# Twelve rotary units that scale at the end on ScalarE, and one operand's splits fenced later, in a two-layer encoder

## The chip, the cores and the metric

The program runs on one core of one Trainium2 chip. The metric is the device time of one execution in microseconds. One execution of the kernel before was also profiled; its lines are what the prediction reads. Engines are named as in the profile: PE (matrix products), PEld (its weight loads), DVE (vector), ACT (scalar, activations), POOL (GpSimd), SP (which issues most of the DMAs).

## The reference, cut to what matters

Two layers over 1024 tokens of 1024 features, in float32. Each layer: RMS norm, one input projection, several attention groups (and a cross-attention to 256 memory tokens), a SiLU gate, an output projection, a residual. The first hunk concerns group A of layer 0, whose queries and keys are normalised for each head and then rotated; the second the output projection of layer 1.

```python
qa = rope_2d(rmsnorm(qa.reshape(B, S, A_HEADS, HEAD_DIM), q_norm_a[e]), grid_row, grid_col)
ka = rope_2d(rmsnorm(ka.reshape(B, S, A_KV, HEAD_DIM), k_norm_a[e]), grid_row, grid_col)
...
def rmsnorm(x, g):
    xf = x.astype(jnp.float32)
    y = xf * lax.rsqrt(jnp.mean(xf * xf, axis=-1, keepdims=True) + EPS)
    return (y * g.astype(jnp.float32)).astype(x.dtype)
...
def _rotate_axis(xa, ang):
    x1, x2 = jnp.split(xa, 2, axis=-1)
    return jnp.concatenate([x1 * c - x2 * s, x1 * s + x2 * c], axis=-1)
...
x = x + y @ w_out_odd[o]
```

The inverse root is one number for each token and head, and the rotation is linear, so the root may be multiplied in before or after it.

## The kernel before, in words

Every matrix product is made of three: an operand is split into a high part (rounded to the product's format, a copy on ACT) and a low part (the operand minus the high part, on DVE or POOL), and high x high, high x low and low x high are added up in a PSUM bank. So each weight tile and each moving operand passes ACT and then DVE or POOL before PE can use it. In the profile `wraw` is a loaded weight, `wh` and `wl` its parts.

The phases follow each other: the preparation (0 to about 145 us: group A's projections, the memory's keys and values, roots), layer 0's attention and output projection, the front of layer 1, layer 1's attention, and layer 1's output projection (from about 1340 us to the end). The instructions are written in program order, but a planner orders them for each engine when the program is built: it simulates the engines, takes ready instructions by priority, which is the program's order changed by the offsets in `AHEAD`, and respects fences, `issue_after(x)`, which keep an instruction behind `x` on that engine's queue. The order is then fixed for each engine, and waits on semaphores do the rest.

The preparation projects group A in units of 256 tokens: four units (k0 to k3) of keys, two heads by two blocks of 128 tokens, that is 4 roots and 256 columns, and eight units of queries (q0 to q7), four heads by two blocks, 8 roots and 512 columns. `a_unit` makes a projection in a bank of PSUM tag `pj` (five banks; the keys' are copied to SBUF tiles `x` first). `rope` then squares it on ACT (`rt1`, two buffers), sums each head on DVE, takes the root (`inv_sqrt`: ACT's Sqrt, then a reciprocal and a step of refinement, four small DVE instructions), multiplies the projection by the root (L890, tile `rqn`), multiplies that by the cosine table (L893) and, half by half, the sine table (L895, tile `rt2`, one buffer), and adds the two on POOL (L898, tile `rp`, two buffers). The sum is kept as `self.rotated`, behind which POOL's first weight splits of layer 0 are fenced. One unit later PE transposes `rp` (`back`) and the result is split. The memory values of layer 1 (L597) run between, on two more `pj` banks.

The output projection multiplies in blocks with seven products of sums, Strassen's way, which take in turn the operands `y11`, `t1`, `t2`, `t3`, `y22`, `y21` and `t4`. `y_parts` loads an operand's six tiles (`SP`) and splits them, each ACT copy and DVE difference behind the fence `after`, a pair (`self.high`, the last weight's high copy, and `self.added`, the last addition of a product to the residual). For layer 1 (`last`) the third operand `t3` lies in tiles H, the fourth `y22` in tiles with the tags P, P, q, q, v, of which P is an alias of k. At `t3` the fence for `y22` is taken right after t3's own splits are written, before t3's weights:

```python
        y = self.y_parts(yd, tags["y"][3], "t3", after, self.fetched if last else None)
        after = self.high, self.added
```

In the loop that follows, each of four products (18 matrix products of 512 columns each) reads two weight tiles of 384 columns, made by `weights` through `w_parts`, whose low parts alternate between DVE and POOL; `closed(i)` loads a residual and adds a bank of the first product to it. The printed functions carry the line numbers of the profile.

Of the kernel before, what the change touches and what calls it, by code (L numbers as in the profile page):

```python
# [13 lines left out]
OP = mybir.AluOpType  # L14
# [50 lines left out]
class Trunk:  # L65
# [802 lines left out]
    def rope(self, src, heads, tables, q):  # L868


        nc = self.nc
        n = 2 * heads
        w = n * 64
        bs = slice(2 * q, 2 * q + 2)
        cg, sg = tables
        s4 = src.rearrange("p b (h d) -> p b h d", d=64)
        t1 = self.st("rt1", [128, 512])[:, :w]
        t4 = t1.rearrange("p (b h d) -> p b h d", b=2, d=64)
        nc.scalar.activation(t4, s4, AF.Square)
        ss = self.st("rss", [128, 8])[:, :n]  # L880
        sv = ss.rearrange("p (b h) -> p b h", b=2)
        nc.vector.tensor_reduce(ss, t1.rearrange("p (a d) -> p a d", d=64), axis=AX.X, op=OP.add)
        big = int(heads == 4)
        nc.vector.scalar_tensor_tensor(sv, sv, 1.0 if big else 1.0 / 64, self.e2[:, big, bs][:, :, None].to_broadcast([128, 2, heads]),
                                       op0=OP.mult, op1=OP.add)
        y = self.inv_sqrt(ss, n)
        yv = y.rearrange("p (b h) -> p b h", b=2)
        qn = self.st("rqn", [128, 512])[:, :w]
        q4 = qn.rearrange("p (b h d) -> p b h d", b=2, d=64)
        nc.vector.tensor_tensor(q4, s4, yv[:, :, :, None].to_broadcast([128, 2, heads, 64]), op=OP.mult)  # L890
        u = self.st("rt2", [128, 512])[:, :w]
        u4 = u.rearrange("p (b h d) -> p b h d", b=2, d=64)
        nc.vector.tensor_tensor(t4, q4, cg[:, bs, None, :].to_broadcast([128, 2, heads, 64]), op=OP.mult)  # L893
        for o, i in ((0, 32), (32, 0)):
            nc.vector.tensor_tensor(u4[:, :, :, o:o + 32], q4[:, :, :, i:i + 32],  # L895
                                    sg[:, bs, None, o:o + 32].to_broadcast([128, 2, heads, 32]), op=OP.mult)
        rp = self.st("rp", [128, 512])[:, :w]
        self.rotated = nc.gpsimd.tensor_tensor(rp, t1, u, op=OP.add)  # L898
        return rp.rearrange("p (b g n) -> p b g n", b=2, n=128)

    def back(self, rp, h, l):
# [424 lines left out]
    def out_project(self, w, sd, yd, res, done, tags, banks, first, begun, last=False):  # L1326
# [4 lines left out]
        nc = self.nc  # L1331
# [3 lines left out]
        def weights(i, kind, us=(0, 1)):  # L1335

            src = sd[i][:, "3124".index(kind[1]), :] if kind[0] == "s" else w[i if kind[1] == "1" else 4 + i][:, 768 * (kind[2] == "2"):]
            for c in (cut[u] for u in us):
                with self.ahead("w"):
                    raw = self.st("wraw", [128, UNIT * 128], pool=self.base, bufs=4)[:, :384]  # L1340
                    self.fetched = nc.sync.dma_start(raw, src[:, c])
                    yield self.w_parts(raw, self.either())

        def product(y, bank, ws, start, cols=slice(0, 512), ks=range(6)):
            for u, (h, l) in enumerate(ws):
                for k in (k for k in range(3) if 3 * u + k in ks):
                    for e, (s, m) in enumerate(((h, 0), (h, 1), (l, 0))):
                        last = nc.tensor.matmul(bank, s[:, k, :], y[3 * u + k][m][:, cols],  # L1348
                                                start=start and u + k + e == 0, stop=u == 1 and k + e == 4,
                                                skip_group_check=True)  # L1350
            return last
# [19 lines left out]
        def residual(x, nt, half):  # L1371
            with self.tc.issue_after(self.fetched.ins) if last else nullcontext():
                nc.sync.dma_start(x, res[nt][:, 512 * (2 - half):512 * (3 - half)])

        def plus(x, p, op=OP.add):
            self.added = nc.vector.tensor_tensor(x, x, p, op=op)

        def square(x, k):

            sq = self.st(self.square_tag if k else "vt", [128, 512])  # L1380
            nc.scalar.activation(sq, x, AF.Square)
            if 0 < k < apart:
                nc.gpsimd.tensor_tensor(sums[0], sums[0], sq, op=OP.add)
            else:
                sums.append(sq)
# [11 lines left out]
        def closed(i):  # L1397
            residual(at(c22, i), 4 + i, 2)
            with self.ahead("sink"):
                plus(at(c22, i), yb[i])  # L1400
# [10 lines left out]
        y = self.y_parts(yd, tags["y"][1], "t1")  # L1411
        for i in products(y, yb, "s1", True, ready, *([opened] if last else [])):
            if not last:
                closed(i)
            if i == 1:
                after = self.high, self.added

        y = self.y_parts(yd, tags["y"][2], "t2", turn)
# [6 lines left out]
        y = self.y_parts(yd, tags["y"][3], "t3", after, self.fetched if last else None)  # L1425
        after = self.high, self.added
        for i in range(4):
            ws = list(weights(i, "s3")) if last else weights(i, "s3")
            if last:
                closed(i)  # L1430
            product(y, xb[i], ws, False)
            residual(at(c21, i), 4 + i, 1)
            with self.ahead("sink"):
                plus(at(c22, i), xb[i])
                plus(at(c21, i), xb[i])
                square(at(c22, i), i)

        y = self.y_parts(yd, tags["y"][4], "y22", after)
        after = self.high, self.added
# [9 lines left out]
        y = self.y_parts(yd, tags["y"][5], "y21", after)  # L1449
        after = self.high, self.added  # L1450
# [15 lines left out]
        y = self.y_parts(yd, tags["y"][6], "t4", after)  # L1466
# [799 lines left out]
```

## Time and profile before

| | |
|---|---|
| median of 3 runs | 1481.07 us |
| lowest, highest | 1480.27, 1485.23 us |
| the profiled execution | 1483.22 us |
| its span, first to last instruction | 1481.4 us |
| PE busy | 1462.3 us, 99% |
| DVE, ACT, POOL busy | 70%, 57%, 44% |
| granted clock of PE, mean | 0.995 |

In the views below, a row of the waits reads: who waited, for whom, microseconds in total, number of times, longest. A row of a timeline or of the chain reads: start, length, engine, line, instruction, tiles out<-in, count; in square brackets the idle time before it and what ended it. A row of busy time by stage reads: length, busy time (and instructions) of PE, PEld, DVE, ACT and POOL, granted clock, share of the DMA engines, GB/s. A row of one line's instructions reads: count, shortest/median/longest duration in ns, first and last start, shapes. A DMA row ends with the median time from issue to landing. Products in PE overlap, so the starts of two neighbours show their true distance, not their durations.

### The profile page before, as it was taken

The numbers are of one execution on the slowest core, as the hardware profiler recorded it, in microseconds if no ns is written. First come the engines' busy times: TensorE is split into PE (matmuls) and PEld (weight loads), VectorE is DVE, ScalarE is ACT, GpSimd is POOL, SyncE is SP. The second block draws the span as 40 slices with busy tenths as digits, with TensorE's granted clock in tenths as the row PEclk, the third lists the DMA queues.
The fourth block names the chain that finished last, engine by engine and source line by source line (L and its number), as shares of the span: only waits on it lengthen the run. The fifth ranks groups of instructions, "written<-read, shape, count | busy, mean of one in ns | idle before, by whom it ended". The sixth has DMA issues, their size and how long they took to land.

```text
span 1481.4 us, 24750 instructions
## 1 busy us (share of the span) xinstructions
PE 1462.3 (99%) x8049; PEld 1257.4 (85%) x8049; DVE 1035.0 (70%) x2125; ACT 838.4 (57%) x1877; POOL 645.1 (44%) x766
## 2 busy tenths in 40 slices
PE   9999999999999999999999999999999999999997
PEld 8998888988888888888888877888888888888786
DVE  6787777777766678776687866654457777787674
ACT  7733665556655356654544444444456777776453
POOL 1223668566765646553450000002325556764354
PEclk9999999999999999999999999999999999999999
DMA  8966335334342524388553434567575567789844
GB/s 279 324 153 181 118 114 169 121 121 138 116 139 83 195 78 142 104 270 308 188 179 127 145 133 143 154 166 276 201 268 172 187 206 255 249 249 325 284 141 141
DMA packets 171809, 271.87 MB, mean 184 GB/s; under 512 B 15648, under 2 KB 92704, under 8 KB 170656
## 3 DMA queue, kind: packets, MB, share of 16 engines
q1 hardware_dynamic: 171248, 270.20, 56.6%
q8 instruction: 64, 1.05, 0.3%
q14 instruction: 65, 0.53, 0.1%
q10 hardware_dynamic: 432, 0.09, 0.0%
HBM read 174.28 MB, written 83.89 MB: 174 GB/s over the span
## 4 chain that ended last, share of the span: by engine, by line
PE 88%; DVE 4%; DMA 3%; ACT 2%; issue 1%; SPq 1%; POOL 1%; POOLq 0%; DVEq 0%; ACTq 0%
PE pj L242 16%; PE pj L62 12%; PE x L1648 7%; PE tr L133 6%; PE pv L1080 4%; PE y L1648 4%; PE pv L62 3%; PE s L62 3%; PE pj L1348 3%; PE tr L62 3%; PE sa L1348 3%; PE pv L1648 2%; PE tr L1348 2%; PE sa L1046 2%; PE sa L1047 2%; PE s L1348 2%
## 5 line engine op out<-in xcount | busy, mean ns | idle before, releaser
L549 DVE TENSOR_TENSOR pl<-tr,ph 128x512 fp32r<-128x512 f32 (+2 forms) x352 | 204.4, 594 | 45.5 <-ACT ph L125 43.5
L242 PE MATMUL pj<-H,wh 128*128 128x512 f32 x704 | 233.5, 412 | 0.5 <-DVE vt L313 0.2
L125 ACT ACTIVATE ph<-tr 128x512 fp32r<-128x512 f32 (+2 forms) x352 | 176.6, 522 | 99.9 <-PE tr L133 78.0
L158 POOL TENSOR_SCALAR wh<-wraw 128x512 fp32r<-128x512 f32 x48 | 30.2, 631 | 270.0 <-PE x L1648 232.9
L125 ACT ACTIVATE wh<-wraw 128x384 fp32r<-128x384 f32 (+1 forms) x163 | 88.8, 553 | 103.3 <-PE pj L1348 17.6
L242 PE MATMUL pj<-H,wl 128*128 128x512 f32 x352 | 139.0, 395 | 0.0
L242 PEld LDWEIGHTS pj<-H,wh 128*128 128x128 f32 x704 | 120.2, 189 | 18.3 <-issue 0.6
L62 PE MATMUL pj<-H,wh 128*128 128x512 f32 x384 | 121.0, 396 | 0.0
L133 PE MATMUL tr<-ident,P 128*128 128x128 f32 x752 | 115.5, 273 | 0.7 <-DVE pl L549 0.3
L1133 POOL TENSOR_SCALAR pn<-pn,st 128x384 f32<-128x384 f32 (+1 forms) x128 | 72.7, 570 | 97.6 <-DVE st L1132 56.5
L1295 POOL TENSOR_TENSOR wl<-wraw,wh 128x384 fp32r<-128x384 f32 x56 | 63.2, 1131 | 98.7 <-ACT wh L125 88.5
L1131 ACT ACTIVATE pn<-pn,st 128x384 f32<-128x384 f32 (+1 forms) x128 | 75.1, 587 | 39.4 <-DVE st L1128 37.8
L133 PEld LDWEIGHTS tr<-ident,P 128*128 128x128 f32 x752 | 88.9, 140 | 9.3 <-POOL P L732 1.6
L1052 ACT ACTIVATE P<-sa,st 128x1024 f32<-128x1024 f32 x64 | 71.5, 1117 | 34.3 <-PE tr L133 19.6
L1054 POOL TENSOR_SCALAR P<-P,st 128x1024 f32<-128x1024 f32 x64 | 74.5, 1166 | 31.3 <-DVE st L1053 31.3
L1051 DVE TENSOR_REDUCE st<-sa 128x1 f32<-128x1024 f32 x64 | 77.6, 1219 | 7.8 <-PE sa L1047 6.8
L62 PE MATMUL s<-k,q 128*128 128x384 f32 (+1 forms) x352 | 81.2, 327 | 0.0
L242 PEld LDWEIGHTS pj<-H,wl 128*128 128x128 f32 x352 | 66.2, 188 | 15.1
L62 PE MATMUL pj<-H,wl 128*128 128x512 f32 x192 | 75.6, 394 | 0.0
L160 POOL TENSOR_TENSOR wl<-wraw,wh 128x512 fp32r<-128x512 f32 x52 | 70.5, 1358 | 9.2 <-ACT wh L125 6.5
L62 PEld LDWEIGHTS pj<-H,wh 128*128 128x128 f32 x384 | 66.6, 188 | 5.4
L864 PE MATMUL pj<-ah,H 128*128 128x256 f32 x384 | 70.5, 282 | 0.0
(574 smaller groups left out, 4171.8 us busy)
## 6 DMA issues: line engine op xcount, KB each, us to landing
y<-yb SPq DMA_DIRECT2D x24, 512.0 KB, 4.1
wraw<-s SPq DMA_DIRECT2D x64, 192.0 KB, 4.3
wraw<-w_e SPq DMA_DIRECT2D x44, 256.0 KB, 3.4
k<-k SPq DMA_DIRECT2D x42, 256.0 KB, 5.8
s<-bias SPq DMA_DIRECT2D x56, 192.0 KB, 2.0
wq<-w_o SPq DMA_DIRECT2D x40, 256.0 KB, 3.4
y<-sg SPq DMA_DIRECT2D x18, 512.0 KB, 3.3
wraw<-w_o SPq DMA_DIRECT2D x36, 256.0 KB, 4.4
```

The lines of the kernel that those rows point to most:

```text
L62: return lambda *a, **k: self.tc.keep_in_program_order(getattr(self.engine, name)(*a, **k))
L125: return self.nc.scalar.activation(out, in_, AF.Copy, scale=scale)
L133: self.turned = self.fence = self.pe.transpose(o, i, self.ident)
L242: self.pe.matmul(a[:, :n], s[:, kt % UNIT, :], m, start=(kt == 0 and i == 0), stop=(kt == KT - 1 and i == 2))
L549: self.low = nc.vector.tensor_tensor(pl[:, :n], tr[:, :n], ph[:, :n], op=OP.subtract)
L1051: nc.vector.tensor_reduce(st[:, 0:1], s, axis=AX.X, op=OP.max, negate=True)
L1052: nc.scalar.activation(pt, s, AF.Exp, bias=st[:, 0:1], accum_out=st[:, 1:2])
L1054: self.normal = nc.gpsimd.tensor_scalar(pt, pt, st[:, 2:3], 0.5, op0=OP.mult, op1=OP.mult)
L1131: nc.scalar.activation(o, o, AF.Exp, bias=st[:, 0:1], scale=-1.0, accum_out=st[:, 2:3])
L1133: self.normal = normal = nc.gpsimd.tensor_scalar(o, o, st[:, 3:4], 0.5, op0=OP.mult, op1=OP.mult)
L1348: last = nc.tensor.matmul(bank, s[:, k, :], y[3 * u + k][m][:, cols], start=start and u + k + e == 0, stop=u == 1 and k + e == 4, skip_gro ...
L1648: self.last = nc.tensor.matmul(bank, ws[s][:, k, :], b[k][m], start=start and k + i == 0, stop=k == UNIT - 1 and i == 2, skip_group_check= ...
```

## The change

In `rope`, the tables multiply the raw projection `s4`; the multiplication by the root and the tile `rqn` for it go. The root is taken after the POOL sum in program order, and ACT multiplies each head and block of the sum (128 x 64) in place by its root: eight copies with a scale for a unit of queries, four for one of keys. `self.rotated` stays the POOL sum. The pool of `rqn` stays, since `rope_tables` uses it. In `out_project` the fence for `y22` is, for layer 1, taken again in the first turn of t3's loop, when the two weight tiles of that turn have been made.

```diff
         big = int(heads == 4)
         nc.vector.scalar_tensor_tensor(sv, sv, 1.0 if big else 1.0 / 64, self.e2[:, big, bs][:, :, None].to_broadcast([128, 2, heads]),
                                        op0=OP.mult, op1=OP.add)
-        y = self.inv_sqrt(ss, n)
-        yv = y.rearrange("p (b h) -> p b h", b=2)
-        qn = self.st("rqn", [128, 512])[:, :w]
-        q4 = qn.rearrange("p (b h d) -> p b h d", b=2, d=64)
-        nc.vector.tensor_tensor(q4, s4, yv[:, :, :, None].to_broadcast([128, 2, heads, 64]), op=OP.mult)
         u = self.st("rt2", [128, 512])[:, :w]
         u4 = u.rearrange("p (b h d) -> p b h d", b=2, d=64)
-        nc.vector.tensor_tensor(t4, q4, cg[:, bs, None, :].to_broadcast([128, 2, heads, 64]), op=OP.mult)
+        nc.vector.tensor_tensor(t4, s4, cg[:, bs, None, :].to_broadcast([128, 2, heads, 64]), op=OP.mult)
         for o, i in ((0, 32), (32, 0)):
-            nc.vector.tensor_tensor(u4[:, :, :, o:o + 32], q4[:, :, :, i:i + 32],
+            nc.vector.tensor_tensor(u4[:, :, :, o:o + 32], s4[:, :, :, i:i + 32],
                                     sg[:, bs, None, o:o + 32].to_broadcast([128, 2, heads, 32]), op=OP.mult)
         rp = self.st("rp", [128, 512])[:, :w]
         self.rotated = nc.gpsimd.tensor_tensor(rp, t1, u, op=OP.add)
+        y = self.inv_sqrt(ss, n)
+        for i in range(n):
+            self.copy(rp[:, i * 64:i * 64 + 64], rp[:, i * 64:i * 64 + 64], y[:, i:i + 1])
         return rp.rearrange("p (b g n) -> p b g n", b=2, n=128)
...
         for i in range(4):
             ws = list(weights(i, "s3")) if last else weights(i, "s3")
             if last:
+                if i == 0:
+                    after = self.high, self.added
                 closed(i)
             product(y, xb[i], ws, False)
```

## The prediction

> **What bounds the kernel now.** I read the page's busy times first, then the waits of PE, then busy time by stage, and last the chain of waits and the timelines of the two places that the diff touches.
>
> ```profile
> span 1481.4 us, 24750 instructions
> PE 1462.3 (99%) x8049; PEld 1257.4 (85%) x8049; DVE 1035.0 (70%) x2125; ACT 838.4 (57%) x1877; POOL 645.1 (44%) x766
> ```
>
> PE is idle for 1481.4 - 1462.3 = 19.1 us in all, so an edit that leaves PE's work as it is can win only from this and from stretches where PE ran slowly. The waits of PE say where:
>
> ```profile
> PE pj L1348 <- ACT wh L125: 2.0, 1, 2.0
> ...
> PE pj L597 <- DVE wl L160: 1.3, 3, 0.8
> ...
> PE pj L597 <- DVE rqn L890: 0.8, 1, 0.8
> ...
> PE tr L133 <- POOL rp L898: 0.4, 1, 0.4
> ```
>
> The first is the longest wait of PE, and it lies in the output projection that the second hunk edits. The other three (1.3 + 0.8 + 0.4 = 2.5 us) lie in the preparation, where the rotary units run. By stage:
>
> ```profile
> 74.00:111.00 37.00, 36.25 (x285) 34.43 (x284) 31.80 (x86) 14.44 (x33) 9.73 (x8) 1.00 0.63 154
> 111.00:148.00 37.00, 35.66 (x209) 30.54 (x209) 26.69 (x57) 13.02 (x25) 12.80 (x13) 1.00 0.65 181
> 1370.00:1407.00 37.00, 34.78 (x141) 27.25 (x140) 22.17 (x31) 16.14 (x32) 14.13 (x11) 0.95 0.85 284
> ```
>
> Columns: length, then PE, PEld, DVE, ACT, POOL busy, granted clock, DMA share. In the preparation DVE is busy for 31.8 of 37 us and ACT for 14.4: DVE is what PE waits for, and ACT has room. In the third row PE also lost clock (0.95).
>
> **Second hunk: the fourth operand's splits.** The chain of waits runs through ACT here:
>
> ```profile
> 1392.62 0.51 ACT wh L125
> 1393.13 1.04 ACT k L125 x2
> 1394.17 0.39 ACT q L125
> ...
> 1395.12 1.14 ACT v L125 x2
> 1396.26 0.58 ACT H L125 x2
> ...
> 1397.72 1.35 ACT wh L125 x3
> ...
> 1399.11 9.75 PE pj L1348 x34
> 1408.86 8.40 PE s L1348 x36
> ```
>
> k, q and v are the buffers of the fourth operand (y22); H is the third (t3), which the next product needs. The six copies of y22 fill ACT from 1393.13 to 1396.26, ahead of three copies of t3 and of the first weights of that product. Their fence is the weight copy of 1392.62, the last of the stage before; the edit makes it the second of the 1397.72 group, so the six go behind t3's copies and the weights that PE waits for. What PE lost, and how slowly it ran after:
>
> ```profile
> 1395.87 0.39 PE L1361 MATMUL s<-H,wl 128*128 128x512 f32 x1
> 1398.28 2.04 PE L1348 MATMUL pj<-H,wh 128*128 128x512 f32 x4 [2.02 <-ACT wh L125]
> ...
> 1408.70 1.09 PE L1348 MATMUL s<-H,wh 128*128 128x512 f32 x4
> ```
>
> ```profile
> 1398.30:1402.70 4.40, 4.29 (x11) 3.15 (x12) 4.40 (x8) 1.17 (x3) 2.32 (x2) 0.61 0.47 130
> 1402.70:1406.70 4.00, 4.00 (x19) 3.23 (x18) 4.00 (x7) 1.19 (x3) 1.01 (x1) 1.00 0.90 283
> ```
>
> 36 products take 8.40 us at full rate (the chain's last row, 0.233 us each). The last of the stage before started at 1395.87, so the next could start at 1396.10 and started at 1398.28: 2.18 us. The 36 from there end at 1408.70, 10.42 us later, 2.02 us more than 8.40: the granted clock was 0.61 after the wait. Together 4.2 us hang on this place.
>
> [...]
>
> Can the first products start at 1396.10? What they need, and when it lands:
>
> ```profile
> 1385.23 2.85 SPq L1251 DMA_DIRECT2D H<-y  x6
> 1388.33 1.06 SPq L1341 DMA_DIRECT2D wraw<-s  x2
> ```
> ```profile
> H<-y SPq DMA_DIRECT2D x2, 256.0 KB, 6.3
> ```
> ```profile
> wraw<-s SPq DMA_DIRECT2D x1, 192.0 KB, 6.0
> ```
>
> The last two loads of t3 (issued up to 1388.08) take 6.3 us by the median: the last lands near 1394.0. The second raw weight goes out at about 1389.1 and lands at 1395.1. ACT, free at 1393.13, then does three t3 copies (0.52 us apart) by 1394.7 and two weight copies by 1395.6: the weights' high parts are in time. Their low part goes to DVE:
>
> ```profile
> 1393.36 0.68 DVE L1376 TENSOR_TENSOR mk<-mk,pj 128x512 f32<-128x512 f32 x1
> 1395.65 0.69 DVE L1376 TENSOR_TENSOR H<-H,tr 128x512 f32<-128x512 f32 x1 [1.61 <-DMA H<-x]
> 1396.26 0.68 DVE L1376 TENSOR_TENSOR mk<-mk,pj 128x512 f32<-128x512 f32 x1
> 1396.85 1.89 DVE L129 TENSOR_TENSOR H<-H 128x512 fp32r<-128x512 f32 x3
> 1398.66 0.55 DVE L1295 TENSOR_TENSOR wl<-wraw,wh 128x384 fp32r<-128x384 f32 x1
> ```
>
> This is what is late next. DVE sits from 1393.96 to 1395.65 in front of a residual's load. If the three t3 differences (0.6 us apart) fall into that hole, the low part follows the two additions, 1396.85 to 1397.40; PE needs it as its third operand at 1396.10 + 2 x 0.233 = 1396.57 and waits 0.8 us. If the low part is placed in the hole too, nothing is lost. If DVE keeps its order, the low part still ends at 1399.2 and nothing is won. So the place gives 0 to 4.2 us; I take the middle order, 4.2 - 0.8 = **3.4 us**, because the planner puts ready work into such a hole and t3's halves are ready at 1393.7 to 1394.7.
>
> The six copies themselves: ACT has 3.4 us free in this row, and y22 is first used as the stage after t3's four products, 72 products or 16.8 us after 1396.1, so they cost nothing. If they delay the next weights (a second pair of copies), these are needed 18 products (4.2 us) later, at 1400.3; behind six copies they end at 1395.6 + 3.1 + 0.9 = 1399.6.
>
> ```profile
> 1402.84 0.53 ACT L125 ACTIVATE wh<-wraw 128x384 fp32r<-128x384 f32 x1 [3.37 <-PE pj L1348]
> ```
>
> **First hunk: rotary units.** Twelve units, four of 256 columns (4 heads by block) and eight of 512 (8). Rows of what goes:
>
> ```profile
> L890 DVE TENSOR_TENSOR rqn<-pj,iq_y x8: 678/692/692, 88.7 to 137.5; 128x512 f32<-128x512 f32 x8
> L890 DVE TENSOR_TENSOR rqn<-x,iq_y x4: 417/422/426, 57.7 to 82.9; 128x256 f32<-128x256 f32 x4
> ```
>
> DVE loses one multiplication a unit: 8 x 0.692 + 4 x 0.422 = 7.2 us, about 6.2 us at the 0.1 us by which neighbours overlap. The three multiplications by the tables stay; they read the projection, mostly in PSUM, where the removed one read it too at 0.69, so I leave their price. What comes is one ACT copy of 128x64 with a scale for each head and block: 8 x 8 + 4 x 4 = 80. Nearest rows:
>
> ```profile
> 55.90 1.28 ACT L125 ACTIVATE va<-x,rs 128x128 fp32r<-128x128 f32 x4
> L792 ACT ACTIVATE iq_t<-rss 128x8 f32<-128x8 f32 x8 | 1.6, 206 | 9.3 <-DVE rss L884 9.3
> L125 ACT ACTIVATE va<-x,rs 128x128 fp32r<-128x128 f32 x8 | 2.6, 391 | 1.7 <-DVE rs L796 1.6
> ```
>
> Four scaled 128x128 copies take 1.28 us, (1.28 - 0.39) / 3 = 0.30 us apart; a 128x8 root takes 0.21 us. 128x64 lies between, nearer the first; I take 0.25 us, so 2.0 us a unit of 512, 1.0 us of 256, and 20 us of ACT in all (17 to 24). ACT has 22.6 and 24.0 us free in the two windows above, so this fits, but it stands in one queue with the weight copies.
>
> Latency of a unit: before, root (0.2 + 4 x 0.17), multiplication 0.69, tables 0.68 + 0.75, sum 1.3 one after the other; now tables and sum run beside the root, and 2.0 us of copies follow. That is a draw, within 0.5 us. But the PSUM bank is let go after the tables without the root, and DVE is shorter by 0.6 us a unit. PE's waits in 100 to 120 us are the bank (0.75), and low parts on a late DVE (0.83, 0.26, 0.17). These 2.0 us can go; the 0.4 us on the k unit's sum can grow by the 1.0 us of its copies. Bounds: +1.5 to -2.5 us; I take half of DVE's share, **-1.0 us**. The last POOL sum, behind which POOL's first weight splits of layer 0 queue, comes earlier by the root and the multiplication; PE has other products there, 0.
>
> **Sum.** 3.4 + 1.0 = 4.4 us off. The profiled execution took 1483.22 us, so 1478.8 by its own time; it stands 2.15 us above the median of the three runs, and the same step on the median gives 1481.07 - 4.4 = **1476.7 us**. What one measurement of this kernel can tell from no change is about 0.3%, 4.4 us.
>
> **The rivals.** (a) DVE keeps its order at the third product, or the clock is not lost in the ordinary run: only 0 to 2 us there, with the preparation's 1.0 a total of 1478 to 1480. For it: the runs spread from 1480.27 to 1485.23, so the half clock may not be in every run; the residual's load is in front of DVE. Against it: six copies of 3.13 us stand in the chain itself. (b) The half clock after 1398.3 has another cause than the wait, and stays: the wait alone goes, 2.2 - 0.8 + 1.0 = 2.4 us, 1478.7. For it: nothing in the rows ties the fall to the wait but their order; against it: the clock is 1.00 again in the row after, and no other wait stands before it. [...] (c) Slower: the scales stand in ACT's queue ahead of the weight copies for the memory values, which PE takes from 102 to 120 us.
>
> ```profile
> ACT wh L125 <- DMA wraw<-w_mem: 10.3, 7, 3.9
> ```
>
> Seven of these copies start as their weight lands; four units' scales (q2 to q5), 2.0 us each, put in front of such copies, are 8 us late at worst. With 3.4 won at the third product that is +4.6, 1485.7. It decides from a delay above 3.4 us, that is from two units in front of a weight that PE needs next. Against it: the planner sends a ready copy between two scales of 0.25 us. (d) The instruction order after the preparation is drawn anew, and elsewhere new waits of 1 to 3 us appear: this eats the gain, 1478 to 1480.
>
> **How the numbers follow.** Both places as summed, or with the DVE hole fully used (4.2 + 2.5 = 6.7, 1474.4): 0.50, of which a little falls short of 0.3%. (a) 0.20, (b) 0.08, (d) 0.13, (c) 0.09. So faster 0.47, same 0.45, slower 0.08. Range: from 1473.5, where all 6.7 us are won and the run lies 0.8 us under the median as the lowest of the three does, to 1482.0, no change and 1 us lost to (c) or (d).
>
> **What would show it.** Right: no wait of PE at L1348 over 1 us near 1396, clock 1.00 there, y22's copies behind the weight copies, DVE's L890 gone, 80 ACT copies of 128x64 near 0.34 us, and fewer waits at L597. Wrong: a wait of L1348 on DVE's low part of 2 us or more; L597 waiting for ACT's weight copies; PE's idle time over 19 us from waits that were not there.

## The result, and the profile after

The changed kernel takes 1488.14 us (median of 6 runs, 1487.16 to 1489.18) against 1482.22 us of the kernel before beside it (6 runs, 1480.27 to 1485.23): ratio 1.0043, 95% interval 1.0032 to 1.0055. It is 6 us slower, where 4.4 us less were forecast. Its profiled execution took 1487.96 us. The ratios below leave out two executions far above the rest, one of the kernel before (6231.81 us) and one of e14 (1591.58 us).

From the page of the changed kernel, the span and the busy times:

```profile
span 1486.2 us, 24828 instructions
PE 1463.4 (98%) x8049; PEld 1255.7 (84%) x8049; DVE 1031.6 (69%) x2113; ACT 856.7 (58%) x1957; POOL 646.6 (44%) x766
```

PE's idle time is 1486.2 - 1463.4 = 22.8 us, 3.7 us more than in the profile of before, with the same 8049 products. ACT has 80 instructions and 18.3 us more. By stage (length; PE, PEld, DVE, ACT, POOL busy; granted clock, DMA share, GB/s):

```profile
74.00:111.00 37.00, 34.96 (x294) 34.51 (x293) 27.88 (x86) 24.62 (x77) 10.84 (x9) 1.00 0.48 129
111.00:148.00 37.00, 34.84 (x191) 29.22 (x190) 20.88 (x46) 18.77 (x53) 10.38 (x9) 0.95 0.70 199
1370.00:1407.00 37.00, 37.00 (x161) 29.74 (x160) 23.13 (x29) 17.55 (x36) 14.76 (x13) 1.00 0.94 325
```

The third row, the place of the second hunk, is full and at full clock. The first two, the preparation, are not full, and the second is at 0.95: DVE is 3.9 and 5.8 us emptier there than before, as the change meant it, ACT 10.2 and 5.8 us fuller, and PE does 1.3 and 0.8 us less. The waits of PE over the whole span, the first lines (who waited, for whom, us in total, times, longest):

```profile
PE tr L133 <- ACT rp L125: 3.0, 3, 1.4
PE tr L133 <- issue: 2.0, 1, 2.0
```

Both are the transposes of the rotated heads (L133), which now wait for the scale. The wait of 2.0 us for the first weights of the third product, at the head of this list before, is gone.

### The profile page after: what moved, and what is told of

It is laid out like the page before. It is cut to its first block, busy times and chain, and to the rows that moved or that the text cites. A ratio compares the mean times of both kernels' runs of the same rounds, so it can differ in the third digit from the quotient of the medians.

```text
span 1486.2 us, 24828 instructions
## 1 busy us (share of the span) xinstructions
PE 1463.4 (98%) x8049; PEld 1255.7 (84%) x8049; DVE 1031.6 (69%) x2113; ACT 856.7 (58%) x1957; POOL 646.6 (44%) x766
## 4 chain that ended last, share of the span: by engine, by line
PE 87%; DVE 4%; DMA 4%; ACT 3%; issue 1%; SPq 1%; POOL 0%; DVEq 0%; ACTq 0%; POOLq 0%
PE pj L242 16%; PE pj L62 12%; PE x L1648 7%; PE tr L133 6%; PE pv L1078 4%; PE y L1648 4%; PE pv L62 3%; PE s L62 3%; PE tr L62 3%; PE pj L1346 3%; PE sa L1346 3%; PE pv L1648 2%; PE s L1346 2%; PE sa L1044 2%; PE sa L1045 2%; PE tr L1346 2%
## 5 line engine op out<-in xcount | busy, mean ns | idle before, releaser
L242 PE MATMUL pj<-H,wl 128*128 128x512 f32 x352 | 139.0, 395 | 0.0
L242 PEld LDWEIGHTS pj<-H,wh 128*128 128x128 f32 x704 | 120.4, 189 | 18.3 <-issue 0.6
L133 PE MATMUL tr<-ident,P 128*128 128x128 f32 x752 | 115.3, 273 | 0.7 <-DVE pl L549 0.3
L133 PEld LDWEIGHTS tr<-ident,P 128*128 128x128 f32 x752 | 88.8, 140 | 9.4 <-POOL P L732 1.3
```

Source lines behind the costliest of these rows:

```text
L133: self.turned = self.fence = self.pe.transpose(o, i, self.ident)
L242: self.pe.matmul(a[:, :n], s[:, kt % UNIT, :], m, start=(kt == 0 and i == 0), stop=(kt == KT - 1 and i == 2))
```

## The second profile of before, and where the time lies

Two numbers of the first profile of before misled. A second one (e12_before_again) shows it, and the rest is easier to read after it.

**e12_before_again**: the kernel before, unchanged.

> The kernel before, unchanged, for a second profile of it. If the half clock behind the third product belongs to one execution and not to the kernel: the wait of TensorE for VectorE near 1394 to 1396 us is there, with the same order, but the clock is 1.00 in the stretch behind it in this profile or the wait is under 1 us, and the span is 1476 to 1479 us. If it belongs to the kernel: wait of 2.18 us, clock 0.81 in the stretch behind it, span 1481 us.

Measured: 1479.83 us (10 runs), ratio to the other runs of the same kernel 0.9995 (0.9987 to 1.0004). The wait of PE at the third product, and two stretches there:

```profile
PE pj L1348 <- ACT wh L125: 0.2, 1, 0.2
```

```profile
1396.00:1400.00 4.00, 3.77 (x15) 2.80 (x16) 4.00 (x8) 1.77 (x5) 2.36 (x2) 1.00 0.39 99
1400.00:1404.00 4.00, 4.00 (x19) 3.26 (x18) 4.00 (x6) 0.61 (x2) 1.21 (x1) 1.00 0.87 257
```

Neither the wait nor the half clock is there, with the same instructions in the same order. The profile of e2 below, whose output projection is that of before, has 0.3 us of wait there. So the 4.2 us on which the second hunk's gain rested aren't in every execution. How many have them isn't shown. Of 113 runs of this kernel beside the experiments none had a mean clock under 0.996, and of the ten here one had 0.995, as the first profile had; but that profile has a second slow stretch (0.72 from 35 to 40 us), and one stretch alone, 1.7 us of 1481, lowers the mean by only 0.001.

**e1_tail**: the kernel before with the second hunk alone.

```diff
             if last:
+                if i == 0:
+                    after = self.high, self.added
                 closed(i)
```

> The kernel before with the second hunk alone (the later fence for the fourth operand's splits); the preparation is that of before. In the trace of the changed kernel the wait of PE on ACT at the third product is gone and the last landmark of PE has moved 3.8 us less than the one before the third product. Theory A (the hunk works as predicted, 3.4 to 4.2 us): 1478.4 us against a kernel before of 1482.2, and the distance from the last product of the second operand to the first 128x1 product of the final sums shorter by 3.8 us. Rival (the half clock after the wait is not in every run, or the gain came from the later start of this stage in the changed kernel): 1480.2 to 1482.

Measured: 1481.66 us (12 runs), ratio 0.9992 (0.9981 to 1.0003). That is 1.2 us less by the ratio and 0.4 by the medians, between 2.8 us less and 0.4 more. The second hunk does no harm, its gain isn't told from none, and the 3.4 us that were forecast lie outside.

**e2_rope**: the kernel before with the first hunk alone (the diff of `rope`).

> The kernel before with the first hunk alone (rotary units on the raw projection, eight ACT copies by the root at the end). Theory A (the two hunks act in separate places and add): 1482.2 + 5.9 + 3.8 = 1492 us, with layer 0's first scores near 148.2 us instead of 143.0, and the wait of 2 us with its half clock at the third product back. Rival (the loss comes from both hunks together, by the order drawn anew): below 1489.

Measured: 1488.53 us (7 runs), ratio 1.0036 (1.0022 to 1.0051). That is 5.3 us (3.3 to 7.6), so the rotary units alone account for the loss. The 1492 us of theory A counted on 3.8 us from the second hunk, which e1 doesn't show. The loss's place in time, busy times of the first 150 us in the second profile of before:

```profile
0.00:150.00 150.00, 144.75 (x1005) 132.70 (x1006) 108.09 (x263) 86.22 (x197) 40.09 (x39) 1.00 0.77 235
```

and of the changed kernel:

```profile
0.00:150.00 150.00, 140.34 (x976) 128.46 (x977) 97.63 (x246) 102.61 (x273) 38.10 (x37) 0.99 0.75 231
```

PE is idle for 5.25 us there before and for 9.66 us after: 4.4 us more, and the clock gives away 1.7 us besides (it is 0.66 from 125 to 130 us): 6.1 us together. The end of the preparation shows the same: the first score product of layer 0 starts at 141.96 us in the second profile of before (142.95 in the first) and at 148.21 in the changed kernel. The table, in the order of the ratios, has 150 minus PE busy for all the kernels, with the first and last start of the memory values' products of layer 1 (L597) on PE:

| kernel | median us | ratio to before (95%) | PE idle in 0 to 150 us | values' products |
|---|---|---|---|---|
| e12 before again | 1479.83 | 0.9995 (0.9987 to 1.0004) | 5.25 | 102.9 to 119.4 |
| e1 second hunk | 1481.66 | 0.9992 (0.9981 to 1.0003) | 4.85 | 102.1 to 119.2 |
| e8 ACT's scale first | 1482.38 | 1.0013 (1.0003 to 1.0023) | 5.03 | 103.0 to 120.8 |
| e7 no scale | 1481.62 | 1.0009 (0.9999 to 1.0018) | 6.60 | 106.6 to 132.1 |
| e9 no scale, w=400 | 1482.43 | 1.0010 (1.0002 to 1.0019) | 6.22 | 107.2 to 120.4 |
| e14 DVE's scale, w=400 | 1485.19 | 1.0020 (1.0008 to 1.0032) | 7.54 | 107.3 to 122.0 |
| e13 six buffers, w=400 | 1485.64 | 1.0024 (1.0013 to 1.0036) | 8.82 | 109.8 to 122.5 |
| e18 later end, w=400 | 1485.06 | 1.0025 (1.0015 to 1.0036) | 7.97 | 106.2 to 121.8 |
| e3 DVE's scale | 1487.11 | 1.0027 (1.0017 to 1.0038) | 8.55 | 106.5 to 134.8 |
| e17 later end | 1485.64 | 1.0033 (1.0021 to 1.0045) | 10.50 | 107.8 to 135.5 |
| e4 six buffers | 1488.01 | 1.0033 (1.0021 to 1.0046) | 10.11 | 105.8 to 136.1 |
| e6 w=400 | 1485.91 | 1.0034 (1.0021 to 1.0048) | 8.01 | 109.2 to 122.5 |
| e2 first hunk | 1488.53 | 1.0036 (1.0022 to 1.0051) | 10.64 | 109.8 to 138.2 |
| e16 root first | 1486.29 | 1.0039 (1.0026 to 1.0052) | 7.80 | 109.6 to 135.0 |
| e10 POOL's scale | 1488.21 | 1.0042 (1.0030 to 1.0054) | 9.61 | 110.9 to 137.0 |
| e11 POOL's scale, w=400 | 1487.44 | 1.0042 (1.0030 to 1.0054) | 10.16 | 111.0 to 125.5 |
| the changed kernel | 1488.14 | 1.0043 (1.0032 to 1.0055) | 9.66 | 108.1 to 136.4 |
| e15 third sum buffer | 1488.94 | 1.0047 (1.0031 to 1.0064) | 8.65 | 107.5 to 139.0 |
| e5 loads held back | 1499.23 | 1.0124 (1.0110 to 1.0139) | 20.97 | 123.9 to 140.4 |

The medians come from several chips, on which before took 1480.15 to 1482.22 us; the ratios compare on one chip. The idle times are of one execution each, in e14 of its fastest (1481.74 us), and they follow the ratios only roughly (10.50 us in e17 at 1.0033, 8.65 in e15 at 1.0047). The first score product parts the kernels better: it starts at 141.7 to 143.6 us in those up to 1.0013, at 145.4 to 150.0 in those from 1.0020 to 1.0047, and at 161.1 in e5.

## What the trace shows in the changed kernel

One unit near 100 us, from the timelines of POOL, DVE, ACT and PE (start, length, instruction; in brackets the idle time before and its releaser):

```profile
98.50 1.29 POOL L893 TENSOR_TENSOR rp<-rt,rt 128x512 f32<-128x512 f32 x1 [1.48 <-PE tr L133]
```
```profile
101.72 0.17 DVE L796 SCALAR_TENSOR_TENSOR iq_y<-iq_t,iq_y 128x8 f32<-128x8 f32 x1
```
```profile
104.35 0.60 ACT L125 ACTIVATE so<-tr 128x512 fp32r<-128x512 f32 x1 [3.33 <-DMA qa<-so]
104.85 2.01 ACT L125 ACTIVATE rp<-rp,iq_y 128x64 f32<-128x64 f32 x8
```
```profile
105.52 0.30 PE L133 MATMUL tr<-ident,rp 128*128 128x128 f32 x1 [2.04 <-issue]
```

The sum ends at 99.79 us, where before the transposes could begin. The root is ready at 101.89. The scale starts at 104.85, because ACT's next instruction in order is the split of another unit, which waits 3.33 us for a store to free its buffer. PE waits 2.04 us, until the first copies of the scale are done (the view finds no releaser and says issue). Near 123 us PE waits for a scale again, 1.36 and 0.56 us, but for another reason: ACT stands free there, and the root is ready only at 122.51, behind a sum that ends at 122.29:

```profile
122.61 2.02 ACT L125 ACTIVATE rp<-rp,iq_y 128x64 f32<-128x64 f32 x8 [2.80 <-DVE iq_y L796]
```

A stretch of low clock follows (0.95 in the stage row above).

SP's queue has changed too. In the second profile of before, six of the eight raw loads of the memory values go out ahead of the 32 stores of the first pair's queries (L941, L942), which follow about 0.64 us apart, and two behind the first 16 of them:

```profile
87.99 0.37 SPq L138 DMA_DIRECT2D wraw<-w_mem  x1
...
92.19 1.13 SPq L138 DMA_DIRECT2D wraw<-w_mem  x1
...
94.77 1.46 SPq L138 DMA_DIRECT2D wraw<-w_mem  x2
...
97.02 2.12 SPq L138 DMA_DIRECT2D wraw<-w_mem  x2
99.19 0.55 SPq L941 DMA_DIRECT2D q<-so  x1
...
110.36 1.17 SPq L138 DMA_DIRECT2D wraw<-w_mem  x2
```

In the changed kernel one load goes ahead, and seven behind all the stores (the first four of them shown):

```profile
94.29 1.21 SPq L138 DMA_DIRECT2D wraw<-w_mem  x1
95.60 1.34 SPq L923 DMA_DIRECT2D k<-k  x1
97.04 0.54 SPq L939 DMA_DIRECT2D q<-so  x1
...
119.08 1.12 SPq L940 DMA_DIRECT2D qa<-so  x1
120.30 2.22 SPq L138 DMA_DIRECT2D wraw<-w_mem  x4
```

So most of the values' products, which ran from 102.9 to 119.4 us, run after 125 us. Between 103 and 125 us PE has less other work while a unit's scale is late. Two theories came of this: Q, the queue of SP is the cause; S, the scale ahead of the transposes is. The experiments were to part them. The expectations of e3 and e4 carry earlier names: B, the loss lies in ACT's queue; C, in the new order; D, in the 2 us of the scale itself.

## The experiments: which of the two

**e3_dve**: the scale at the end by one instruction of DVE, so ACT's queue is as before.

```diff
-        for i in range(n):
-            self.copy(rp[:, i * 64:i * 64 + 64], ...)
+        r3, y3 = rp.rearrange("p (a d) -> p a d", d=64), y[:, :, None].to_broadcast([128, n, 64])
+        nc.vector.tensor_tensor(r3, r3, y3, op=OP.mult)
```

> The changed kernel, but the sum is multiplied by the roots in one DVE instruction (128x512, by broadcast) instead of eight ACT copies; both hunks otherwise as changed. Theory B (the loss lies in ACT's queue: the eight copies stand behind ACT copies that wait for the stores of the queries, and PE's transposes behind them): the transposes no longer wait for ACT, the preparation takes about what it took before (first scores near 143 to 144 us), 1478 to 1480 us. Rival C (the loss lies in the new order, with the products for the memory values behind all rotary units): first scores stay near 148 us, 1486 to 1489 us.

Measured: 1487.11 us, ratio 1.0027. About 4 of the 6 us stay with nothing added to ACT, so B fails as the whole cause; the time lies in C's range. Its longest wait of PE in the preparation:

```profile
PE pj L597 <- ACT wh L125: 2.5, 1, 2.5
```

**e4_so6**: six store buffers `so` instead of four, so that ACT's wait of 3.33 us goes.

```diff
-            ... rp=2, so=4, ...
+            ... rp=2, so=6, ...
```

(To make room the raw sine table lies in `rt1`.)

> The changed kernel with six buffers instead of four for the tiles in which the split queries wait for their stores (room made by loading the raw sine table into a buffer of the squares instead of a tile of its own). Theory B (scales queue on ACT behind copies that wait for a store): the waits of ACT and DVE for these stores (5.3 and 7.8 us) go, and with them most of the 5 us in which PE waited at the transposes: 1482 to 1485 us. Rival D (the 2 us of eight copies after the sum are the loss, whatever stands before them): the transposes wait as before, 1487 to 1489 us.

Measured: 1488.01 us, ratio 1.0033, not the gain of B. The wait near 105 us is gone, which D didn't expect, and another stands at 125 us for weights that lie behind the stores:

```profile
PE pj L597 <- ACT wh L125: 3.5, 2, 3.1
PE tr L133 <- ACT rp L125: 2.3, 3, 1.0
```

**e5_late**: before, with the eight raw loads held behind the last store.

```diff
+                self.loaded = self.stored    # the last store of pair 0
                 self.mem_values(w1m, mem, kvd[1], "so")()
+                self.loaded = None
```

> The kernel before, its rotary units untouched, with one thing added: the eight raw loads of the second layer's memory values are issued behind the last of the 32 stores of the first pair's queries on SP's queue, as seven of the eight are in the changed kernel. Theory Q (SP's queue: the loads behind the stores are what starves TensorE near 105 to 126 us, about 4 to 5 of the 6 us): 1486 to 1488 us, the values' products (L597) end near 134 to 138 us and not at 120. Theory S (the end of each unit, which now waits for root and scale ahead of its transposes, is the cost): 1482 us, within 1 us of before.

Measured: 1499.23 us, ratio 1.0124, 18 us: three times what Q expected and more. PE's waits:

```profile
PE pj L597 <- ACT wh L125: 10.1, 1, 10.1
PE tr L133 <- POOL rp L898: 7.6, 3, 3.5
```

The order on SP's queue can cost far more than the change did, even without any scale. That it can isn't that it did.

**e6_w400**: the changed kernel, the head start of weights in the planner 400 instead of 40. The eight loads now go out behind at most five of the 32 stores.

```diff
-    "prep": dict(w=40),
+    "prep": dict(w=400),
```

> The changed kernel, with the planner's head start for weights in the preparation at 400 instead of 40, which puts seven of the eight raw loads ahead of all but a few of the 32 stores on SP's queue. Rotary units and scales as in the changed kernel. Theory Q: 1482 to 1484 us, the first loads of the values land near 100 us, their products end near 122 us. Theory S: 1487 to 1488.5 us, the waits of the transposes for the scales stay and so does the loss.

Measured: 1485.91 us, ratio 1.0034. The loads are early and the products end at 122.5 us, yet the loss is all but whole, so Q falls as the single cause. The wait is at the scale again. ACT's copies wait for these loads (2.32, 0.71 and 0.96 us between 99 and 106 us), now ahead of the scale, and DVE's splits for ACT's copies (2.24, 0.57 and 1.31 us), ahead of the root; the scale starts at 106.81 us:

```profile
PE tr L133 <- issue: 3.5, 1, 3.5
```
```profile
106.53 0.16 DVE L796 SCALAR_TENSOR_TENSOR iq_y<-iq_t,iq_y 128x8 f32<-128x8 f32 x1
```

**e7_noscale**: the changed kernel without the 80 copies; the heads stay unscaled.

```diff
-        for i in range(n):
-            self.copy(rp[:, i * 64:i * 64 + 64], ...)
```

> The changed kernel without the scaling of the heads: roots are made, the 80 copies on ScalarE are left out. The transposes wait for the sum on POOL alone. SP's queue still holds 32 stores ahead of seven of the eight raw loads. Theory Q: 1485 to 1488 us, slow although work is gone. Theory S: 1481 to 1482.5 us, no slower than before.

Measured: 1481.62 us, ratio 1.0009 (0.9999 to 1.0018). The stores stand ahead of the loads here too, and the loss is 1.3 us (0 to 2.7). This speaks for S, with a limit: without the scale nothing waits for the root either, so the unit's chain is shorter than it was before.

**e8_first**: before with the second hunk, and the 80 ACT copies in place of L890, that is ahead of the tables.

```diff
-        nc.vector.tensor_tensor(q4, s4, yv..., op=OP.mult)
+        for i in range(n):
+            self.copy(q4[:, i // heads, i % heads], s4[...], y[:, i:i + 1])
```

> The kernel before with the second hunk, and the scaling of the heads by their roots moved from one instruction of VectorE to the eight or four copies of ScalarE, in the old order: scaled first, then multiplied by the tables. ScalarE has the same 80 copies as in the changed kernel and the chain to the transposes is longer than in either; of the eight raw loads five stay ahead of the stores. Theory Q: 1481.5 to 1484 us. Theory S: 1486 to 1489 us.

Measured: 1482.38 us, ratio 1.0013 (1.0003 to 1.0023). The same work on the same queue costs 1.9 us ahead of the tables and 6.4 us behind the sum. S as it was worded (ACT's copies in the chain) expected 1486 to 1489 here and falls too: root, copies, tables and sum follow each other, the longest chain of all, and PE's largest wait for it is small:

```profile
PE tr L133 <- POOL rp L899: 0.7, 2, 0.5
```

What is left is the place: an operation that is the last one ahead of the transposes. With the place the order on SP's queue changed too (five of the eight loads are ahead of the stores here), but by e6 that order isn't the cause by itself.

**e9_noscale_w400**: no scale, and the head start of 400.

> The changed kernel with both suspects taken away: the 80 scaling copies are left out (so the heads are not scaled by their roots), and the planner's head start for weights in the preparation is 400, so that the raw loads stand ahead of most of the stores on SP's queue. Theory T (two queues: the scale stands on ScalarE behind instructions that wait for transfers, and what it makes late holds the stores and the loads behind them on SP's queue): within 1.5 us of the kernel before, first scores of the first pair (L1042 to L1045) near 142 us, no wait of TensorE over 1 us between 95 and 126 us. Rival N (the planner's new order of the unit costs by itself, whatever stands in the queues): 3 us or more above before.

Measured: 1482.43 us, ratio 1.0010, 1.5 us above before: at the edge of T's range and outside N's. With the scale gone, the order on SP's queue is worth nothing that can be told.

**e10_pool**: the scale by one POOL instruction behind POOL's own sum.

```diff
+        r4 = rp.rearrange("p (a d) -> p a d", d=64)
+        nc.gpsimd.tensor_tensor(r4, r4, y[:, :, None].to_broadcast([128, n, 64]), op=OP.mult)
```

> The changed kernel with the scaling done by one GpSimd instruction of 128x512 (128x256 for a key unit) behind GpSimd's own sum, in place of the eight or four copies on ScalarE. GpSimd stood idle 9.9 us ahead of its sums near 100 us. 32 stores still stand ahead of the loads. Theory T: 1.5 to 4 us above before, the wait of 2.04 us near 105 us gone or under 1 us, first scores between 143.5 and 146 us. Rival N: 5 to 7 us above before, as the changed kernel.

**e11_pool_w400**: the same with the head start of 400.

> The run before this one, with the planner's head start for weights in the preparation at 400 as well. Theory T: within 1.5 us of the kernel before, either way; first scores near 142 to 143 us. Rival N: 4 us or more above before.

Measured: 1488.21 and 1487.44 us, both ratios 1.0042, in N's range and not in T's. Theory T named the 3.33 us in ACT's queue, and a scale on another engine should have shown it. But the trace of e10 has a longer wait of the same kind:

```profile
107.56 0.60 ACT L125 ACTIVATE so<-tr 128x512 fp32r<-128x512 f32 x1 [6.74 <-DMA q<-so]
```

POOL's scale of this unit ended at 105.42 us. Its transposes started only at 108.79, released by ACT's copies `rows`, which read the transposes' banks (`tr`) and stand behind this split. So the transposes still hung on a store through ACT's queue, by another way, and e10 doesn't clear that queue. PE's waits of e10 are spread over the unit's whole tail:

```profile
PE pj L597 <- ACT wh L125: 1.6, 1, 1.6
PE tr L133 <- ACT rows L125: 1.4, 1, 1.4
PE tr L133 <- POOL rp L896: 0.9, 1, 0.9
```

So a scale behind the sum costs 4 us on DVE, 6.4 on ACT and 6.2 on POOL.

## The experiments: why the place costs

Three causes were left: (1) two waits that cover each other, ACT's store buffer near 105 us and the loads near 125 us; (2) the sum's buffer, held through the scale; (3) the root, worked out on DVE behind the tables.

**e13_so6_w400** and **e14_dve_w400** take both waits of cause 1 away (the edits of e4 and e6, and of e3 and e6).

> The changed kernel with six store buffers and the planner's head start for weights in the preparation at 400: both at once, each of which alone left the loss (1.0033 and 1.0034). Cause 1 (two waits that cover each other): within 2 us of before, TensorE's idle time between 100 and 130 us under 2 us. Otherwise, if the scale behind the sum costs in a third place: 4 us or more above before.

> The scale at the end by one instruction of VectorE, as in e3_dve, where the wait of 2.49 us for the values' weights near 125 us was the largest, with the head start of 400 as well. Cause 1: within 1.5 us of before, that wait gone. Otherwise 3 us or more above before, with the wait at another place.

Measured: 1.0024 (1.0013 to 1.0036) and 1.0020 (1.0008 to 1.0032). By the middle values e13 gives 1.9 of the 4.3 thousandths back, e14 0.7 of e3's 2.7; the intervals overlap those of the single edits. With 3.6 us above before e13 lies between its two ranges, and e14 with 3.0 us where its second one begins. The wait moved once more. In e13 it is the root's turn; from DVE's timeline:

```profile
101.76 0.19 DVE L793 RECIPROCAL iq_y<-iq_t 128x8 f32<-128x8 f32 x1
104.60 0.69 DVE L160 TENSOR_TENSOR wl<-wraw,wh 128x512 fp32r<-128x512 f32 x1 [2.64 <-ACT wh L125]
105.20 0.16 DVE L794 TENSOR_TENSOR iq_t<-iq_y 128x8 f32<-128x8 f32 x1
...
107.26 0.16 DVE L796 SCALAR_TENSOR_TENSOR iq_y<-iq_t,iq_y 128x8 f32<-128x8 f32 x1
```

Four instructions that take 0.7 us together are drawn out over 5.7 us, since weight splits that wait for their load stand between them; then come the scale, and a wait of PE of 2.9 us.

**e15_rp3** (cause 2): three sum buffers.

```diff
-            ... p_tr=3, rp=2, so=4, ...
+            ... p_tr=3, rp=3, so=4, ...
```

> The changed kernel with three buffers for the sum instead of two. Cause 2 (the sum's buffer is held through the scale until the transposes, and the next sum waits for it): 3 us or more of the 6 come back, 1482 to 1484.5 us against 1481.5 of before. Otherwise 1486 to 1488.5 us.

**e16_rootfirst** (cause 3): `y = self.inv_sqrt(ss, n)` back ahead of the products with the tables.

> The changed kernel with the root worked out ahead of the products with the tables, as before; the scale stays at the end, on ScalarE. Cause 3 (the root comes late on VectorE): 3 us or more of the 6 come back. Otherwise 1486 to 1488.5 us.

Measured: 1.0047 and 1.0039. Neither is the cause by itself; in e16 PE still waits 2.21 us for the scale at 105.44 us. No kernel here has six store buffers, early loads and an early root at once, so whether the three waits together are the whole loss stays untested.

**e17_later** and **e18_later_w400**: the end of a unit one unit later, with three sum buffers; the second with the head start of 400.

```diff
-            if len(late) > 1:
+            if len(late) > 2:
```

> The changed kernel with three sum buffers, and the end of each rotary unit (transposes, split, stores) put two units behind its start instead of one. If the end comes too early for the scale: TensorE's waits for the scale near 105 and 123 us under 0.5 us each, 2 to 4 us of the 6 back, 1483.5 to 1485.5 us; a rest stays, since 24 stores still stand ahead of the loads. If slack does nothing: 1487 to 1489 us.

> The same with the planner's head start for weights in the preparation at 400. If the end comes too early for the scale: within 1.5 us of before, TensorE's idle time between 100 and 130 us under 1.5 us. If slack does nothing: 4 us or more above before, as with the head start alone.

Measured: 1.0033 (1.0021 to 1.0045) and 1.0025 (1.0015 to 1.0036): 1.5 and 2.7 of the 6.4 us come back by the middle values, less than the slack was to give. Waits of PE in e17 and then in e18:

```profile
PE pj L597 <- ACT wh L125: 2.7, 1, 2.7
```
```profile
PE tr L133 <- issue: 1.9, 1, 1.9
```

Shown: the loss arises in the first 150 us, with the scale as the last operation ahead of the transposes, on any of three engines; without it, or with it ahead of the tables, 1.3 to 1.9 us are lost by the middle values. Also shown, by the rows: near 105 us of the changed kernel PE waits for a scale that stands behind an instruction waiting for a transfer, and each edit that frees one such place leaves a wait at another. Only argued: that the reason is the order in which the planner puts the unit's tail. It fits that e8's units have the longer chain and no such wait, and that e8's values' products start at 103.0 us, as before's do, while those of every kernel with a scale at the end start at 105.8 to 111.0 us; but those of e7 and e9 start at 106.6 and 107.2 us too and lose little, so a late start alone doesn't do it. Not settled: the 3 to 3.7 us that stay in e13, e14 and e18, and how much of the loss of POOL's scale is the wait for a bank behind ACT's split. No version here beats the kernel before beyond what can be told; e1 comes nearest.

## Why the prediction was wrong, by its steps

- **The bound.** Right in kind: PE is full, and only its idle time and clock could move. The idle time grew to 22.8 us, which the prediction had named as the sign of being wrong ("over 19 us from waits that were not there").
- **Second hunk, -3.4 us.** This term failed. It was priced from the timeline and the clock of one execution; the second profile has 0.2 us of wait and a clock of 1.00 at the same place, and e1 measured 1.2 us by its ratio, not told from 0. Rival (a) had the right half of it ("the clock is not lost in the ordinary run"), and the spread of the three runs was rightly taken as a hint. The profiled execution stood 2.15 us above its median. That was the other hint, and it was carried into the sum as if it had no place. What was forecast of the order came: in the changed kernel y22's copies stand behind the weight copies, no wait over 1 us is left there and the clock is 1.00. But before had neither in its second profile, so this doesn't show what the edit is worth. Whether the wait took the clock stays open, as the second profile has neither.
- **First hunk, prices.** Right. The 80 copies, in the groups of ACT's instructions:

```profile
L125 ACT ACTIVATE rp<-rp,iq_y 128x64 f32<-128x64 f32 x80 | 20.4, 335 | 7.3 <-DVE iq_y L796 7.2
```

  335 ns was forecast as 0.34 us, eight take 2.01 us where 2.0 were, and ACT gained 18.3 us where 20 were. The table products cost the same from the raw projection (medians 0.68 and 0.41 us for 512 and 256 columns, 0.68 and 0.42 from the scaled tile before). DVE's loss is 6.0 us by the prediction's own figures (7.2 less twelve overlaps of 0.1), not 6.2; its busy time fell by 3.4 us against the first profile and by 8.3 against the second. Nothing hung on it.
- **First hunk, -1.0 us with +1.5 as the upper bound.** This is the step that failed most; it measured +5.3 us alone (e2) and 6.4 with both hunks. "That is a draw, within 0.5 us" compared the durations of a unit's instructions and let the root run beside the tables and the sum, so that the copies could start at the sum's end. The trace has 7.1 us between the sum's end (99.79) and the scale's last copy (106.86), of which 2.0 are the scale's own: the root, on DVE behind the tables and a weight split, was ready 2.1 us after the sum, and the copies then stood 3.0 us in ACT's queue. No term of the sum held such a wait. "ACT has room" was true (24.62 of 37 us busy) and beside the point: room is a mean, and the scale waited in order behind a split that waited 3.33 us for a store. "DVE is what PE waits for" was half true: DVE came free and PE waited more.
- **First hunk, the waits at L597.** 2.1 us of them were to go, and 0.4 us were left, in the changed kernel's list. They were replaced by waits at the transposes. The 0.4 us on the k unit's sum, which could grow by 1.0 us, became 1.1.
- **Rival (c), slower.** It had the queue and the side, and the wrong direction: scales were to delay weight copies. In the trace copies and splits that wait for transfers delay the scales (e6, and the rows at 104.35), and the weights are late because their loads are issued behind the stores. Its price, 8 us late less the 3.4 won, was against a gain that wasn't there. Its condition, two units in front of a needed weight, was not met: no wait of L597 for ACT's copies is over 0.2 us in the changed kernel.
- **Rival (d), the order drawn anew.** It named the means, a new order, but placed it after the preparation and priced it at 1 to 3 us. In the preparation itself the order on SP's queue was drawn anew, which the prediction didn't look at.
- **Busy time and place.** DVE was busy for 31.8 of 37 us before and lost 3.9, which the prediction took for a gain. Both moves of that work to the end of the unit, ACT's and POOL's, cost 6 us (ACT's ahead of the tables 1.9); DVE's own scale in the same place cost 4. Here the place in the unit set the time, not the share of busy time.

## What to carry to other kernels

An operation that is moved to be the last before PE's operand is to be priced by what stands in front of it in its engine's queue and waits for a transfer (3.33 us here), and by what PE has to do meanwhile, and not by its duration (2.01 us) or the engine's mean load (24.62 of 37 us). List for each queue, the DMA-issuing one too, which instructions with a transfer behind them may come in between. A gain that rests on a wait and a clock in one profiled execution wants a second profile, above all where that execution is slower than its median (by 2.15 us here).

## What the runs showed of the hardware

SP issued the stores of 64x256 about 0.64 us apart, so 32 of them, with a few waits between, held the loads behind them from 97.04 to 120.30 us; holding all eight loads behind them cost 18 us (e5), with PE idle for 20.97 of the first 150 us and a granted clock of 0.92 there.

The granted clock did not follow the length of one wait. In the changed kernel it stayed at 1.00 through the stage with the wait of 2.04 us (74 to 111 us) and was 0.95 in the stage with 1.36 and 0.56 us (111 to 148 us), 0.66 from 125 to 130 us. These two waits and the four transposes around them make 3.2 us without another product (121.97 to 125.20 us). Before had 0.61 behind 2.02 us in one execution. In e13 products of 256 columns started 0.12 us apart behind a wait of 2.90 us (109.31 to 109.66 us), and the clock of the first 150 us was 1.00; in e16 they started 0.21 us apart behind 2.21 us (108.13 to 109.20 us) and 0.12 again from 110.98 us on. What takes the clock isn't shown.
